# Start addresses of the high and low parts of a split-float matmul, moved to fixed remainders of 256 bytes

## The chip, the cores and the metric

The kernel runs on one core of one Trainium2 chip. The metric is the time of one execution in microseconds (us) on the device: 736.43 us is the median of three runs before the change (734.82 to 740.46). A core has 128 partitions of on-chip memory; every address below is a byte address within a partition, and "remainder" always means the address modulo 256.

## The reference

Two blocks of a network run one behind the other on 256 tokens of width 1024: a hybrid mixer with three attentions and a convolutional feed-forward, then a gated linear attention and a dilated window attention. Nearly all the arithmetic lies in products of the 256 x 1024 activations with weight matrices:

```python
z = h @ w_in                                      # first block, 6 + 24 column groups of 128..256
merged = gates0*(ya @ w_branch[0]) + ...          # three branches, then merged @ w_out
a, g = jnp.split(h @ w_up, 2, axis=-1)            # feed-forward, 2816 wide
y = (gelu(conv(a)) * g) @ w_down
proj = x @ gla_w_in;  out = (o * silu(g)) @ gla_w_out     # second block, first layer
kv = x @ w_kv;  proj = x @ swa_w_in;  out = (o * silu(g)) @ swa_w_out   # second layer
```

## The kernel before

**Split products.** A float32 operand is held as two tiles of a shorter float type that TensorE (PE) takes at full rate: a high part (the value rounded) and a low part (the rest). A product is then three matmuls, low x high, high x low and high x high, added up in the same accumulator; the low x low term is left out. `mm3` (line 265) issues these three; they are called a triple here. In a matmul one operand stands (its 128 x 128 block is loaded into the array first by a weight load, PEld, that runs while the matmul before it streams) and the other one moves (256 or 512 columns are streamed through).

**Weights.** `Stream` fetches each weight chunk (2048 floats a partition) by DMA into `raw`, and for each 1024 of them makes `whi` (ScalarE, ACT, line 158) and `wlo` (VectorE, DVE, line 159), each out of six rotating buffers. They are used in two ways:

- *Weights stand* (`wstat`, `wpair`, the first loop, `branch`): 128 x 128 blocks of `whi`/`wlo` stand, 256 columns of the activations move. The order of a triple is (`wlo` stands, high moves), (`whi` stands, low moves), (`whi` stands, high moves). Keys of such chunks are in the list `STILL`.
- *Weights move* (`tokmm`): 128 x 128 blocks of the activations stand, 512 columns of `whi`/`wlo` move. The order is (low stands, `whi` moves), (high stands, `wlo` moves), (high stands, `whi` moves).

**Activations.** The names are those of the trace: `hhi/hlo` (first mixer's input), `yhi/ylo` (attention outputs), `mhi/mlo` (merged), `h2hi/h2lo` (feed-forward's input), `fhi/flo` (its inner activations), `x2hi/x2lo` and `ohi/olo` (gated linear attention), `x3hi/x3lo` and `shi/slo` (window attention). `h`, `m`, `h2`, `x2` and `x3` come out of `big8` (line 397), which takes one of two buffers of the tag `big8r` and starts `past` floats into it. The triples are, by the loops:

| stage | moves or stands | triples |
|---|---|---|
| h: first loop 8 x 12, `inc` 16, `zg` 12 x 16 | moves, 256 columns | 304 |
| y: 3 branches x 8 x 2 | moves, 256 | 48 |
| h2: 22 `up` chunks x 16 | moves, 256 | 352 |
| x2: `gla` 8, four `gk` x 16 | moves, 256 | 72 |
| x3: three `kvk` x 16, sixteen `sq` x 16 | moves, 256 | 304 |
| m 32, f 88, x2 64, o 32, s 32 | stands, 512 weight columns move | 248 |
| x3: `kvv` | stands, 512 or 256 weight columns move | 32 |

**Where tiles lie.** A pool lays its tiles one behind the other; `Lines` rounds each tile up to whole 128 bytes. So a tile that is an odd multiple of 128 bytes long puts the next one at remainder 128. Before the change the `big8r` buffers are 8320 bytes (32.5 x 256): the first starts at remainder 0 and the second at 128. The `wlo` buffers are 4224 bytes (16.5 x 256): they start at 0 and 128 in turn, and where weights stand, 64 bytes further. `whi` buffers are 4096 bytes and all start at 0.

**Order.** The order of the instructions on each engine is set by the code's order, by priorities and by queues written out (`Queue`, `issue_after`). Semaphores tell an engine when a tile is ready or a buffer free.

Of the kernel before, what the change touches and what calls it, by code (L numbers as in the profile page):

```python
# [9 lines left out]
F32R = mybir.dt.float32r  # L10
# [8 lines left out]
S = 256  # L19
D = 1024  # L20
KK = 8
# [11 lines left out]
SC_SWA = float(128.0 ** -0.5)  # L33


STILL = ("in1", "inc", "zg", "br", "up", "gla", "gk", "kvk", "sq")

COLS = {}

# [63 lines left out]
class Stream:  # L103
# [31 lines left out]
    def _chunk(self, i):  # L135
        nc = self.nc
        key, ap, n, part = self.items[i]
        if part < 0:
            raw = self.early.tile([128, n], F32, tag="early", name="early", bufs=3)
        else:  # L140
            raw = self._raw()
        if not part:
            for o in range(0, n, 1024):
                nc.sync.dma_start(raw[:, o:o + 1024], ap[:, o:o + 1024])
            self.done.append(raw)
            return
        nc.sync.dma_start(raw[:, :n], ap)
        parts = []
        for o in range(0, n, part) if part > 0 else range(0, -part, 1024):
            m = min(part, n - o) if part > 0 else min(1024, -part - o)  # L150
            hi = self.pool.tile([128, 1024], F32R, tag="whi", name="whi", bufs=self.hlbufs)
            lo = self.pool.tile([128, 1056], F32R, tag="wlo", name="wlo", bufs=self.hlbufs)
            lo = lo[:, 16:1040] if key[0] in STILL else lo[:, 0:1024]
            with ExitStack() as st:
                for ins in self.behind:
                    st.enter_context(self.tc.issue_after(ins))
                st.enter_context(self.tc.high_priority(self.pri))
                i0 = nc.scalar.activation(hi[:, :m], raw[:, o:o + m], AF.Copy)  # L158
                i1 = nc.vector.tensor_sub(lo[:, :m], raw[:, o:o + m], hi[:, :m].bitcast(F32))  # L159
                self.last = (i0.ins, i1.ins)  # L160
            parts.append((hi, lo))
        self.done.append((part, parts) if part > 0 else (raw, (1024, parts)))
# [68 lines left out]
def hybrid_blocks(ctx, tc, A, out, dbg=None):  # L231
# [3 lines left out]
    cn = Lines(ctx.enter_context(tc.tile_pool(name="cn", bufs=1)), sm)  # L235
# [3 lines left out]
    def open_pool(name):  # L239
        st = ExitStack()  # L240
        p = st.enter_context(tc.tile_pool(name=name, bufs=1))
        return Lines(p, st.enter_context(tc.tile_pool(name=name + "s", bufs=1))), st.close
# [4 lines left out]
    def acc_t():  # L247

        return [ps.tile([128, 512], F32, tag="acc", name="acc", bufs=4) for _ in range(2)]

    def mm_t():
        return ps.tile([128, 512], F32, tag="mm", name="mm", bufs=2)
# [4 lines left out]
    def dump(name, t):  # L257
        if dbg and name in dbg:
            nc.gpsimd.dma_start(dbg[name], t)
# [135 lines left out]
            mm(pr[:, 256 + b:257 + b], ssq[:, b * 128:(b + 1) * 128], ones[:, 0:1], h == 0 and b == 0, h == 3, True)  # L395

    def big8(dt, name, past=0):
        t = cn.tile([128, KK * S + 32], dt, name=name, tag="big8r", bufs=2)
        return t[:, past:past + KK * S].rearrange("p (k s) -> p k s", k=KK)

    hT = (big8(F32R, "hhi"), big8(F32R, "hlo"))
    qk = [acc_t(), acc_t()]
    vps = [mm_t(), mm_t()]
    qci = [at_t(), at_t()]
# [105 lines left out]
    p1, close_p1 = open_pool("p1")  # L510
# [11 lines left out]
    def wpair(key, a, fresh=False):  # L522


        w = ws.get(key)
        p = mm_t()
        if fresh:
            for n in range(2):
                o = p[:, n * 256:(n + 1) * 256]
                W = [wsl(w, n * 1024 + k * 128, n * 1024 + (k + 1) * 128) for k in range(KK)]  # L530
                for k, l in enumerate(W):
                    mm(o, l[1], a[0][:, k, :], k == 0, False)
                    mm(o, l[0], a[0][:, k, :], False, False)
                for k, l in enumerate(W):
                    mm(o, l[0], a[1][:, k, :], False, k == KK - 1)
            return p
        for n in range(2):
            wstat(p[:, n * 256:(n + 1) * 256], w, n * 1024, a)
        return p
# [29 lines left out]
    p = wpair(("inc", 0), hT)  # L569
# [53 lines left out]
                               compare_op=OP.is_ge, fill=NEG, base=0, channel_multiplier=1)  # L623


    yT = (p1.tile([128, 6, S], F32R, name="yhi", tag="yhi"), p1.tile([128, 6, S], F32R, name="ylo", tag="ylo"))
    MC = {}
    hs = lambda h: (h % 2) * 2 + h // 2
    hb = lambda p, h, K: p[h % 2][:, h // 2 * 256:h // 2 * 256 + K]
# [146 lines left out]
    for i in range(2):  # L776
        w = ws.get(("br", i))
        for u in range(4):
            n = 4 * i + u
            p = mm_t()  # L780
# [6 lines left out]
        if i:  # L787
            w2 = ws.get(("br", 2))
            branch2(0)
            branch2(1)  # L790
        gates(9 + 2 * i)
    mT = (big8(F32R, "mhi"), big8(F32R, "mlo"))
    for i in range(4):
        if i > 1:
# [107 lines left out]

    close_p1()
    close_p1a()
    res, _ = open_pool("res")
    ctx.callback(_)
    p2, close_p2 = open_pool("p2")
    wk = p2
    xn = p2.tile([128, 2, D], F32, name="xn")
# [3 lines left out]

    rms_residual(y, xn, mod[0], x1, ORD1, (xr, mod[2]))
    dump("x1", x1)
    h2 = (big8(F32R, "h2hi"), big8(F32R, "h2lo", 16))

    def ev_h2(j, p, act, dve):
        for low in range(2):
# [76 lines left out]
    for i in range(4):  # L996
        p = wpair(("gk", i), x2T)
# [193 lines left out]
    xqt = p3.tile([128, 2, D], F32, name="lnw", tag="sg")  # L1191
    layer_norm(x2, y3, row("lng0"), None, x3, lambda i: (xkt, xqt)[i // 2][:, i % 2, :], ORD3)
    dump("x3", x3)
    x3T = (big8(F32R, "x3hi", 8), big8(F32R, "x3lo", 24))

    def ev_x3(j, p, act, dve):
        for low in range(2):
# [16 lines left out]
            nc.scalar.dma_start(x3d[b], x3[:, b, :])  # L1214

    close_p3()
    p4, close_p4 = open_pool("p4")
    ctx.callback(close_p4)
    wk = p4
# [3 lines left out]
    for i in range(3):  # L1223
        p = wpair(("kvk", i), x3T, i == 0)
# [84 lines left out]
    for h in range(8):  # L1309
# [8 lines left out]
        if h == 2:  # L1318
# [3 lines left out]
            for a in range(4):  # L1322
                for b in range(4):
                    q = (a % 2) * 64 + b * 16
# [119 lines left out]
```

## Time and profile before

| | |
|---|---|
| median of the runs | 736.43 us (734.82 to 740.46) |
| the profiled execution | 733.62 us, its span 731.6 us |
| PE busy | 700.6 us, 96% of the span |
| DVE, ACT, POOL busy | 547.1, 407.1, 20.2 us |
| mean granted clock of TensorE | 0.986 |

The profile's page sums busy time by engine. The timeline gives each matmul with its start and its duration; durations overlap, as matmuls are pipelined, so the pace of PE is the distance from one start to the next: the difference of two starts over the number of matmuls between them. The windows view gives busy time and the granted clock of a stretch. All starts are microseconds from the span's start.

### The profile page before, as it was taken

Reading aid. Unit: us, or ns where it says so; the run is one execution under the profiler, and the core shown is the slowest. Engines: PE = TensorE matmul, PEld = TensorE weight load, DVE = VectorE, ACT = ScalarE, POOL = GpSimd, SP = SyncE. Lnnn points to the kernel's source line nnn. Section 1 sums busy time; section 2 is a strip of 40 time slices with the busy share of each in tenths; the row PEclk is TensorE's granted clock in tenths of the full one; section 3 lists DMA queues with packets and bytes.
Section 4 is the critical chain, followed back from the end, with each engine's and each line's share of the span. In section 5 each row is a group of like instructions: output and inputs, shape, how many; then the busy total and the mean of one; then the engine's idle time right before and its main releaser. Section 6 shows DMA issues by size and latency. Waiting matters only on the chain. (4 is left out here: it accounts for less than half of the span.)

```text
span 731.6 us, 12192 instructions
## 1 busy us (share of the span) xinstructions
PE 700.6 (96%) x4878; PEld 636.4 (87%) x4878; DVE 547.1 (75%) x933; ACT 407.1 (56%) x675; POOL 20.2 (3%) x34
## 2 busy tenths in 40 slices
PE   4999999999979999999999899999989999999995
PEld 4888888998859999998999797888879999999984
DVE  5877969898868776768566756675777689777866
ACT  3447788546548555554545774543555556555542
POOL 0001000000010000000000200001010000000000
PEclk8999999999999999999999999999999999999999
DMA  8996768677734765758554464231437755433201
GB/s 321 418 345 237 275 257 301 229 250 255 256 136 174 276 243 178 262 207 310 201 195 174 181 224 141 109 116 58 189 142 276 261 194 168 168 125 135 89 1 57
DMA packets 24600, 148.74 MB, mean 203 GB/s; under 512 B 2992, under 2 KB 3248, under 8 KB 9568
## 3 DMA queue, kind: packets, MB, share of 16 engines
q1 hardware_dynamic: 21888, 139.05, 52.1%
q0 software_dynamic: 1280, 5.18, 2.1%
q10 hardware_dynamic: 1376, 3.74, 1.5%
q8 instruction: 38, 0.62, 0.3%
q14 instruction: 18, 0.15, 0.1%
HBM read 145.86 MB, written 2.10 MB: 202 GB/s over the span
## 5 line engine op out<-in xcount | busy, mean ns | idle before, releaser
L159 DVE TENSOR_TENSOR wlo<-raw,whi 128x1024 fp32r<-128x1024 f32 (+1 forms) x193 | 231.3, 1210 | 63.1 <-ACT whi L158 63.1
L158 ACT ACTIVATE whi<-raw 128x1024 fp32r<-128x1024 f32 (+1 forms) x193 | 199.4, 1050 | 94.1 <-PE acc L262 42.5
L262 PE MATMUL mm<-h2hi,wlo 128*128 128x256 f32 x352 | 98.3, 280 | 0.0
L262 PE MATMUL mm<-h2hi,whi 128*128 128x256 f32 x352 | 98.1, 280 | 0.0
L262 PE MATMUL mm<-h2lo,whi 128*128 128x256 f32 x352 | 97.0, 282 | 0.0
L262 PE MATMUL mm<-x3hi,wlo 128*128 128x256 f32 x304 | 86.2, 285 | 0.0
L262 PE MATMUL mm<-x3hi,whi 128*128 128x256 f32 x304 | 85.1, 281 | 0.0
L262 PE MATMUL mm<-x3lo,whi 128*128 128x256 f32 x304 | 82.9, 280 | 0.0
L262 PEld LDWEIGHTS mm<-h2hi,wlo 128*128 128x128 f32 x352 | 67.0, 190 | 0.4
L262 PEld LDWEIGHTS mm<-h2hi,whi 128*128 128x128 f32 x352 | 66.9, 190 | 0.0
L262 PEld LDWEIGHTS mm<-h2lo,whi 128*128 128x128 f32 x352 | 65.1, 188 | 0.3
L262 PE MATMUL mm<-hhi,wlo 128*128 128x256 f32 x208 | 59.5, 286 | 0.5 <-DVE wlo L159 0.3
L262 PE MATMUL mm<-hlo,whi 128*128 128x256 f32 x208 | 59.2, 285 | 0.0
L262 PE MATMUL mm<-hhi,whi 128*128 128x256 f32 x208 | 58.7, 282 | 0.0
L262 PEld LDWEIGHTS mm<-x3hi,wlo 128*128 128x128 f32 x304 | 57.7, 190 | 0.0
L262 PEld LDWEIGHTS mm<-x3hi,whi 128*128 128x128 f32 x304 | 57.5, 189 | 0.0
L262 PEld LDWEIGHTS mm<-x3lo,whi 128*128 128x128 f32 x304 | 56.2, 188 | 0.0
L262 PEld LDWEIGHTS mm<-hhi,wlo 128*128 128x128 f32 x208 | 39.0, 188 | 2.5 <-PE mm L262 0.8
L262 PEld LDWEIGHTS mm<-hlo,whi 128*128 128x128 f32 x208 | 39.1, 188 | 0.8 <-issue 0.8
L262 PEld LDWEIGHTS mm<-hhi,whi 128*128 128x128 f32 x208 | 39.1, 188 | 0.6 <-issue 0.5
L445 DVE SCALAR_TENSOR_TENSOR adacc<-raw,cact,adacc 128x1024 f32<-128x1024 f32 x28 | 35.7, 1276 | 0.2
L262 PE MATMUL acc<-whi,flo 128*128 128x512 f32 x88 | 34.8, 395 | 0.0
(355 smaller groups left out, 1604.0 us busy)
## 6 DMA issues: line engine op xcount, KB each, us to landing
raw<-in_w_up_dram SPq DMA_DIRECT2D x22, 1024.0 KB, 4.9
raw<-in_w_ada_dram SPq DMA_DIRECT2D x16, 1024.0 KB, 4.9
raw<-in_swa_q_dram SPq DMA_DIRECT2D x16, 1024.0 KB, 4.9
raw<-in_w_zg_dram SPq DMA_DIRECT2D x12, 1024.0 KB, 4.9
raw<-in_w_dn_dram SPq DMA_DIRECT2D x11, 1024.0 KB, 4.7
raw<-in_w_ada_dram SPq DMA_DIRECT2D x16, 512.0 KB, 9.0
early<-in_w_in_dram SPq DMA_DIRECT2D x8, 1024.0 KB, 7.3
raw<-in_gla_vg_dram SPq DMA_DIRECT2D x8, 1024.0 KB, 5.1
```

The lines of the kernel that those rows point to most:

```text
L158: i0 = nc.scalar.activation(hi[:, :m], raw[:, o:o + m], AF.Copy)
L159: i1 = nc.vector.tensor_sub(lo[:, :m], raw[:, o:o + m], hi[:, :m].bitcast(F32))
L262: return pe.matmul(o, l, r, start=start, stop=stop, skip_group_check=share)
L445: dve.scalar_tensor_tensor(a, w, c, a, op0=OP.mult, op1=OP.add)
```

## The change

High parts start at remainder 0 everywhere. Low parts of weights that stand start at remainder 64, low parts of activations that move at 192, all others at 0. For this the `wlo` buffers grow to 4352 bytes (17 x 256) and the `big8r` buffers to 8448 (33 x 256), so that every rotating buffer starts at the same remainder; `big8` gets the number of floats to start past (48, that is 192 bytes) for `h`, `h2` and `x3`; the `y` tiles get 256 bytes more, and their low part starts 192 bytes in. For room, the pool `res` (it holds `x2`, 8192 bytes) is closed before the pool of the last stage opens.

```diff
+PAST = 48
...
-            lo = self.pool.tile([128, 1056], F32R, tag="wlo", name="wlo", bufs=self.hlbufs)
+            lo = self.pool.tile([128, 1088], F32R, tag="wlo", name="wlo", bufs=self.hlbufs)
             lo = lo[:, 16:1040] if key[0] in STILL else lo[:, 0:1024]
...
     def big8(dt, name, past=0):
-        t = cn.tile([128, KK * S + 32], dt, name=name, tag="big8r", bufs=2)
+        t = cn.tile([128, KK * S + 64], dt, name=name, tag="big8r", bufs=2)
         return t[:, past:past + KK * S].rearrange("p (k s) -> p k s", k=KK)
 
-    hT = (big8(F32R, "hhi"), big8(F32R, "hlo"))
+    hT = (big8(F32R, "hhi"), big8(F32R, "hlo", PAST))
...
-    yT = (p1.tile([128, 6, S], F32R, name="yhi", tag="yhi"), p1.tile([128, 6, S], F32R, name="ylo", tag="ylo"))
+    yT = tuple(p1.tile([128, 6 * S + 64], F32R, name=n, tag=n)[:, q:q + 6 * S].rearrange("p (k s) -> p k s", k=6)
+               for n, q in (("yhi", 0), ("ylo", PAST)))
...
-    res, _ = open_pool("res")
-    ctx.callback(_)
+    res, close_res = open_pool("res")
...
-    h2 = (big8(F32R, "h2hi"), big8(F32R, "h2lo", 16))
+    h2 = (big8(F32R, "h2hi"), big8(F32R, "h2lo", PAST))
...
-    x3T = (big8(F32R, "x3hi", 8), big8(F32R, "x3lo", 24))
+    x3T = (big8(F32R, "x3hi"), big8(F32R, "x3lo", PAST))
...
     close_p3()
+    close_res()
     p4, close_p4 = open_pool("p4")
```

The remainders of the operands in the two built programs:

| stage | high, low of the activations before | after | `wlo` before | after |
|---|---|---|---|---|
| h (weights stand) | 0, 128 | 0, 192 | 64 and 192 in turn | 64 |
| y (weights stand) | 0, 0 | 0, 192 | 64 and 192 in turn | 64 |
| h2 (weights stand) | 0, 192 | 0, 192 | 64 and 192 in turn | 64 |
| x2 (weights stand) | 128, 0 | 0, 0 | 64 and 192 in turn | 64 |
| x3 (weights stand) | 32, 224 | 0, 192 | 64 and 192 in turn | 64 |
| m (weights move) | 128, 0 | 0, 0 | 0 and 128 in turn | 0 |
| x2 (weights move) | 128, 0 | 0, 0 | 0 and 128 in turn | 0 |
| f, o, s (weights move) | 0, 0 | 0, 0 | 0 and 128 in turn | 0 |
| x3 (weights move) | 32, 224 | 0, 192 | 0 and 128 in turn | 0 |

`whi` is at 0 before and after. Nothing is moved in the order: the rows of all five engines are the same in the two programs, and so are the semaphores and values that each instruction waits for and adds to.

## Rows read from the trace of the kernel before

**Rows 1.** The page: span, and busy time of each engine.

```profile
span 731.6 us, 12192 instructions
...
PE 700.6 (96%) x4878; PEld 636.4 (87%) x4878; DVE 547.1 (75%) x933; ACT 407.1 (56%) x675; POOL 20.2 (3%) x34
```

**Rows 2.** PE's waits, longest first: us in total, times, longest us.

```profile
PE acc L890 <- DVE x L193: 4.1, 3, 2.7
PE mm L262 <- DVE cact L373: 3.7, 1, 3.7
```

**Rows 3.** Windows of h2 with f, x3: stretch, us, busy (x count), PEclk, DMA share, GB/s.

```profile
238.00:395.00 157.00, 157.00 (x1139) 147.40 (x1138) 110.03 (x145) 81.86 (x113) 1.10 (x2) 1.00 0.64 228
...
542.00:594.00 52.00, 52.00 (x389) 49.86 (x388) 39.91 (x52) 32.20 (x46) 1.13 (x2) 0.98 0.72 249
594.00:700.00 106.00, 105.98 (x837) 102.83 (x836) 84.58 (x162) 62.45 (x103) 0.00 (x0) 1.00 0.38 134
```

**Rows 4.** Timeline, h2 stage (start us, us, instruction): first and last of 96 matmuls.

```profile
260.49 0.28 PE L262 MATMUL mm<-h2hi,wlo 128*128 128x256 f32 x1
...
271.48 0.28 PE L262 MATMUL mm<-h2hi,whi 128*128 128x256 f32 x1
```

**Rows 5.** Timeline, x3 stage: first and last of 144, then of 47 matmuls.

```profile
577.16 0.28 PE L262 MATMUL mm<-x3hi,wlo 128*128 128x256 f32 x1
...
594.02 0.28 PE L262 MATMUL mm<-x3hi,whi 128*128 128x256 f32 x1
...
639.10 0.28 PE L262 MATMUL mm<-x3lo,whi 128*128 128x256 f32 x1
...
644.53 0.28 PE L262 MATMUL mm<-x3hi,whi 128*128 128x256 f32 x1
```

**Rows 6.** Timeline, y stage: first and last of 47 matmuls.

```profile
144.61 0.28 PE L262 MATMUL mm<-ylo,whi 128*128 128x256 f32 x1
...
150.03 0.28 PE L262 MATMUL mm<-yhi,whi 128*128 128x256 f32 x1
```

**Rows 7.** Timeline, h stage: matmuls 1, 48, 50, 73 and 96 of 96.

```profile
150.15 0.28 PE L262 MATMUL mm<-hhi,wlo 128*128 128x256 f32 x1
...
155.58 0.28 PE L262 MATMUL mm<-hhi,whi 128*128 128x256 f32 x1
...
156.34 0.28 PE L262 MATMUL mm<-hlo,whi 128*128 128x256 f32 x1
...
159.10 0.28 PE L262 MATMUL mm<-hhi,wlo 128*128 128x256 f32 x1
...
161.81 0.28 PE L262 MATMUL mm<-hhi,whi 128*128 128x256 f32 x1
```

**Rows 8.** Timeline, x2 stage, weights stand: first and last of 165 matmuls.

```profile
418.89 0.28 PE L262 MATMUL mm<-x2hi,wlo 128*128 128x256 f32 x1
...
438.21 0.28 PE L262 MATMUL mm<-x2hi,whi 128*128 128x256 f32 x1
```

**Rows 9.** Timeline, f stage, weights move: first and last of 24 matmuls.

```profile
255.02 0.40 PE L262 MATMUL acc<-whi,flo 128*128 128x512 f32 x1
...
260.26 0.39 PE L262 MATMUL acc<-whi,fhi 128*128 128x512 f32 x1
```

**Rows 10.** Timeline, m stage, weights move: first and last of 94 matmuls.

```profile
191.43 0.40 PE L262 MATMUL acc<-whi,mhi 128*128 128x512 f32 x1
...
213.01 0.39 PE L262 MATMUL acc<-whi,mhi 128*128 128x512 f32 x1
```

**Rows 11.** Timeline, x2 stage, weights move: first and last of 24 matmuls.

```profile
438.33 0.39 PE L262 MATMUL acc<-whi,x2lo 128*128 128x512 f32 x1
...
443.65 0.40 PE L262 MATMUL acc<-whi,x2hi 128*128 128x512 f32 x1
```

**Rows 12.** Groups within 524.78:526.05, o stage, `wlo` at remainder 0: busy us, mean ns.

```profile
L262 PE MATMUL acc<-wlo,ohi 128*128 128x512 f32 x2 | 0.8, 389 | 0.0
```

**Rows 13.** Groups within 526.14:527.45, o stage, `wlo` at remainder 128.

```profile
L262 PE MATMUL acc<-wlo,ohi 128*128 128x512 f32 x2 | 0.8, 395 | 0.0
```

## The prediction

> **What bounds the kernel now.** I read the page first. PE is busy for 700.6 of 731.6 us [rows 1]; no other engine comes near. The waits view then says how much of the rest is waiting: the two longest entries of PE are 4.1 us and 3.7 us [rows 2], at a transition between layers and at the start, and the change touches neither. In the windows of the two stages with the most triples PE is busy without a gap: 157.00 of 157.00 us where h2 and f alternate, 52.00 of 52.00 and 105.98 of 106.00 us in x3 [rows 3]. So the time of these stages is the number of matmuls times the distance from one start to the next, and whatever shortens that distance comes off the end; there is no cover under which it could be lost.
>
> The distances are what the timeline is for. The reader is to see that they differ between stages in which the same instruction runs (128 x 128 standing, 256 moving columns):
>
> - h2: (271.48 - 260.49) / 95 = 115.7 ns [rows 4]
> - x3: (594.02 - 577.16) / 143 = 117.9 ns, and (644.53 - 639.10) / 46 = 118.0 ns [rows 5]
> - y: (150.03 - 144.61) / 46 = 117.8 ns [rows 6]
> - x2: (438.21 - 418.89) / 164 = 117.8 ns [rows 8]
>
> and, with 512 moving columns, f: (260.26 - 255.02) / 23 = 227.8 ns [rows 9], m: (213.01 - 191.43) / 93 = 232.0 ns [rows 10], x2: (443.65 - 438.33) / 23 = 231.3 ns [rows 11]. The clock does not make the difference: it is granted at 1.00, the upper level, in the h2 window and in the later x3 window alike [rows 3].
>
> **Why I put it down to addresses.** Within one stretch of the o stage, same instruction, same neighbours, the matmul that streams `wlo` takes 389 ns when the buffer starts at remainder 0 [rows 12] and 395 ns when it starts at 128 [rows 13]. Nothing else alternates there with the buffer. The size fits too: f, whose operands are all at 0 in this stretch, is the fastest of the moving-weight stages; m and x2, where the high part stands at 128, are the slow ones. With standing weights the layout (high 0, low 192, `wlo` 64 or 192) is h2's, and h2 is the fastest.
>
> [...]
>
> **The change part by part.** It removes, adds and moves no instruction, and no wait changes. What is left is the pace of each stage under its new remainders.
>
> - *x3, weights standing, 304 triples.* It gets h2's layout. At h2's pace a triple saves 3 x (117.9 - 115.7) = 6.6 ns; all 304 would save 2.0 us. The 48 `kvk` triples run in long stretches, and I give them all of it, 0.3 us. The 256 `sq` triples run in pieces of 48 matmuls with plain float32 matmuls between them, and the h stage shows that the pace after such a break depends on more than the addresses (next point). I give them two thirds of 256 x 3 x 2.3 ns = 1.8 us, 1.2 us. Together 1.5 us; bounds 0 and 2.1.
> - *h, 304 triples, low part from 128 to 192.* With unchanged addresses h shows three paces: (155.58 - 150.15) / 47 = 115.5 ns, then, after a wait, (159.10 - 156.34) / 23 = 120.0 ns with `wlo` at 64 and (161.81 - 159.10) / 23 = 117.8 ns with `wlo` at 192 [rows 7]. [...] If half the stretches run well and half as the mean of the two bad ones, 118.9, the stage runs at 117.2; all at h2's 115.7 would save 304 x 3 x 1.5 = 1.4 us, all at 120.0 would cost 304 x 3 x 2.8 = 2.6 us. h2 shows no bad stretch in its windows, but it is hardly ever broken up by float32 matmuls, so I take only 0.4 us.
> - *y, 48 triples, low part from 0 to 192.* 48 x 3 x (117.8 - 115.7) = 0.3 us at h2's pace; I take 0.2.
> - *x2, weights standing, 72 triples, high from 128 to 0, low at 0.* The nearest rows are y's, which has high and low at 0, and y runs at 117.8 like x2. I take 0; bounds 0 and 72 x 3 x 2.1 = 0.5 us.
> - *h2, 352 triples.* Only `wlo` changes, from 64 and 192 in turn to 64. The 96 matmuls of rows 4 hold both kinds and make one pace of 115.7. I take 0.
> - *m and x2, weights moving.* They get f's layout. m: 32 x 3 x (232.0 - 227.8) = 0.4 us. x2: 64 x 3 x (231.3 - 227.8) = 0.7 us. Bounds 0 and 1.1 for both.
> - *f, o, s.* About half of the 64 triples of o and s and a dozen of f's 88 have `wlo` at 128 now; each saves the 6 ns of rows 12 and 13: 44 x 6 = 0.3 us.
> - *x3, weights moving, 32 triples.* High goes from 32 to 0, low stands at 192, where none stood before. Between nothing and f's pace (the like of m, 0.4 us) I take 0.2.
> - *Tiles that only lie elsewhere.* `whi` and all behind `big8r` move by 256 bytes and more, the last pool by the freed 8192 bytes. No remainder of theirs changes and no wait is added: 0.
>
> Sum: 1.5 + 0.4 + 0.2 + 0.4 + 0.7 + 0.3 + 0.2 = 3.7 us. The profiled execution took 733.62 us and would take 729.9. It is 2.8 us below the median of the runs; the same 3.7 us off the median of 736.43 give **732.7 us**.
>
> **The rivals.**
>
> *Nothing happens* (736.4 us). [...] For it: the stages with high pace are those with float32 matmuls between. Against it: 577 to 594 us is a long stretch without such breaks and runs at 117.9 [rows 5], and the 389 and 395 ns alternate within one stretch. [...]
>
> *The new layout falls into the bad step* (slower). The h stage runs at 115.5 and at 120.0 with the same remainders, `wlo` at 64 among both; the change puts `wlo` at 64 in all stages. If x3, y and h, all broken up by float32 matmuls, settled at 120.0, it would cost 304 x 3 x 2.0 = 1.8 us in x3, 48 x 3 x 2.2 = 0.3 in y and 2.6 in h; the moving weights would still give back 1.6. That is 3.1 us slower, 739.5 us. It decides once these 656 triples run more than 1.6 us / 1968 = 0.8 ns slower than now. Against it: h2's fastest pace holds with `wlo` at 64 as well as at 192, and it has a distance of 64 between the streams where h has 128.
>
> *Every conflict goes* (much faster). With `wlo` at 0, f's distance of 227.8 for 512 columns is about 2 x 113.9. If x3, h, y and x2 ran at 113.9 for 256 columns, they would save 304 x 3 x 4.0 + 304 x 3 x 3.3 + 120 x 3 x 3.9 = 8.1 us, with 1.6 us of the moving weights 9.7 us: 726.7 us. Against it: h2 has this layout already and runs at 115.7.
>
> **How the numbers follow.** Forecast 0.72, nothing 0.12, bad step 0.09, much faster 0.07. The best bounds of the parts add up to 2.1 + 1.4 + 0.3 + 0.5 + 1.1 + 0.3 + 0.4 = 6.1 us, 730.3; the runs' median itself can lie a little lower, their lowest is 1.6 us under it, so the range begins at 729.3. Upwards it reaches over "nothing" to 736.5 and leaves out the bad step and the much faster case, 0.16 together. About 1%, 7.4 us, is what a measurement of this kernel can tell from no change. Faster by more than that takes the much faster case or a lucky median: 0.10. Slower by more than that takes more than the bad step: 0.03. The rest, 0.87, is within 1%.
>
> **What would show it right or wrong.** Right: the long x3 stretch near 575 to 592 us falls from 117.9 to about 115.7 ns, m and x2 with moving weights from 232 to about 228, h2 stays at 115.7, and the `wlo` matmuls of o take 389 ns in every buffer. The steps that could fail: the 48-matmul pieces of x3 may stay at 118 or go to 120 after their float32 breaks; h may go either way; the busy windows may be unchanged although the remainders are. The prediction as a whole is wrong if h2, whose layout stays, changes its pace, since then something other than the remainders of 256 matters (the 256-byte shift of `whi` against the activations, for one).

## The result and the profile after

The changed kernel takes 741.92 us (740.6 to 746.53, nine runs) against 736.9 us (734.82 to 740.46, nine runs) of the kernel before on the same chip: a ratio of 1.008 with a 95% interval of 1.0064 to 1.0097. It is 0.8% slower, 9.2 us above the predicted 732.7 and 5.4 us above the range's upper end. The profiled execution took 741.92 us with a span of 739.9. That is 8.3 us more span than before; 3.3 us of this belong to the profiled execution of before, which was that much shorter than the median of its runs, and 5.0 us are the difference of the medians.

The page, against [rows 1]: 8.6 us more busy time on PE with the same 4878 matmuls.

```profile
span 739.9 us, 12192 instructions
...
PE 709.2 (96%) x4878; PEld 646.1 (87%) x4878; DVE 547.3 (74%) x933; ACT 407.8 (55%) x675; POOL 20.1 (3%) x34
```

The longest waits of PE (us in total, times, longest us) are those of [rows 2] to the tenth, and all of PE's waits together come to 21.8 us, against 22.2 before. So the loss is not in the waits:

```profile
PE acc L893 <- DVE x L195: 4.1, 3, 2.7
PE mm L264 <- DVE cact L375: 3.7, 1, 3.7
```

The windows of the three stretches of [rows 3], shifted by what has accumulated: PE is still busy throughout, and the granted clock is 1.00 in all three.

```profile
242.00:402.00 160.00, 160.00 (x1130) 150.26 (x1129) 108.75 (x143) 81.91 (x113) 1.10 (x2) 1.00 0.62 222
550.00:601.00 51.00, 51.00 (x381) 48.50 (x381) 39.65 (x52) 31.75 (x45) 1.13 (x2) 1.00 0.71 249
601.00:709.00 108.00, 107.97 (x844) 104.74 (x843) 84.97 (x163) 62.72 (x104) 0.00 (x0) 1.00 0.37 132
```

So the time is again in the distances. The timeline (start us, us, instruction), as in [rows 4 to 11]:

h2, first and last of 96 matmuls: (275.66 - 264.25) / 95 = 120.1 ns, where [rows 4] gave 115.7. Nine of the ten long stretches of h2 run at 120.0 or 120.1; the first, which begins with another order of its matmuls, runs at 119.5 (before: 116.0 in the first, 115.7 in the others).

```profile
264.25 0.28 PE L264 MATMUL mm<-h2hi,wlo 128*128 128x256 f32 x1
...
275.66 0.28 PE L264 MATMUL mm<-h2hi,whi 128*128 128x256 f32 x1
```

x3, the long stretch of 144: (601.43 - 584.90) / 143 = 115.6 ns, where [rows 5] gave 117.9. Then twelve float32 matmuls, and the 47 behind the first: (608.94 - 603.42) / 46 = 120.0, where [rows 5] gave 118.0. The same tiles, the same remainders, and the first two `wlo` buffers of the two stretches are the very same ones (addresses 133696 and 129344 in the built program): two paces. The other long stretch of x3, 129 matmuls up to 568.02, runs at 119.5, where it ran at 117.7.

```profile
584.90 0.28 PE L264 MATMUL mm<-x3hi,wlo 128*128 128x256 f32 x1
...
601.43 0.28 PE L264 MATMUL mm<-x3hi,whi 128*128 128x256 f32 x1
601.55 1.92 PE L264 MATMUL at<-skT,sq 128*128 128x256 f32 x12
603.22 0.36 PE L264 MATMUL mm<-x3hi,wlo 128*128 128x256 f32 x1
603.42 0.28 PE L264 MATMUL mm<-x3lo,whi 128*128 128x256 f32 x1
...
608.94 0.29 PE L264 MATMUL mm<-x3hi,whi 128*128 128x256 f32 x1
```

y, 48 matmuls: (151.52 - 145.88) / 47 = 120.0, was 117.8 [rows 6]. h, the 48 behind it: (157.28 - 151.63) / 47 = 120.2, was 115.5 [rows 7].

```profile
145.88 0.28 PE L264 MATMUL mm<-yhi,wlo 128*128 128x256 f32 x1
...
151.52 0.28 PE L264 MATMUL mm<-yhi,whi 128*128 128x256 f32 x1
151.63 0.28 PE L264 MATMUL mm<-hhi,wlo 128*128 128x256 f32 x1
...
157.28 0.28 PE L264 MATMUL mm<-hhi,whi 128*128 128x256 f32 x1
```

m, 94 matmuls with moving weights: (215.08 - 193.97) / 93 = 227.0, was 232.0 [rows 10]. x2, 24 of them: (452.02 - 446.78) / 23 = 227.8, was 231.3 [rows 11]. x2 with standing weights, from 427.35 to 446.66 with 165 matmuls, stays at 117.7 [rows 8].

```profile
193.97 0.40 PE L264 MATMUL acc<-whi,mhi 128*128 128x512 f32 x1
...
215.08 0.39 PE L264 MATMUL acc<-whi,mhi 128*128 128x512 f32 x1
...
446.78 0.40 PE L264 MATMUL acc<-whi,x2lo 128*128 128x512 f32 x1
...
452.02 0.39 PE L264 MATMUL acc<-whi,x2hi 128*128 128x512 f32 x1
```

The o stage: the groups of lines within 532.60:534.00, and the same row word for word in the stretch behind it, 534.00:535.40. The 395 of [rows 13] has become the 389 of [rows 12] in both.

```profile
L264 PE MATMUL acc<-wlo,ohi 128*128 128x512 f32 x2 | 0.8, 389 | 0.0
```

The stages with moving weights thus did what was forecast. The loss lies where weights stand, and most of it in h2, the stage whose activations were left where they were.

### The profile page after: what moved, and what is told of

It reads as the page before. It is cut to its first block, busy times and chain, and to the rows that moved or that the text cites. A ratio compares the mean times of both kernels' runs of the same rounds, so it can differ in the third digit from the quotient of the medians.

```text
span 739.9 us, 12192 instructions
## 1 busy us (share of the span) xinstructions
PE 709.2 (96%) x4878; PEld 646.1 (87%) x4878; DVE 547.3 (74%) x933; ACT 407.8 (55%) x675; POOL 20.1 (3%) x34
## 5 line engine op out<-in xcount | busy, mean ns | idle before, releaser
L264 PE MATMUL mm<-h2hi,whi 128*128 128x256 f32 x352 | 100.0, 285 | 0.0
L264 PE MATMUL mm<-h2hi,wlo 128*128 128x256 f32 x352 | 99.9, 285 | 0.0
```

The source lines that it names most:

```text
L264: return pe.matmul(o, l, r, start=start, stop=stop, skip_group_check=share)
```

## The experiments

**How to read the tables.** A stage is the part of the kernel that multiplies one activation (h, y, h2 and so on). A pace is the distance from start to start in ns, taken over each stretch of at least 40 matmuls that nothing interrupts, and averaged over a stage's stretches. A pace of 115.7 is 347 ns a triple, 117.8 is 353, 120.0 is 360: steps of about 6.7 ns a triple. Layouts are written (high, low; `wlo`), remainders of the operands with standing weights; `whi` is always at 0. A ratio is the time over that of the kernel before, run alongside (medians 737.0, 737.35 and 738.28 us), with its 95% interval behind it. The granted clock is 1.00 around all lines of h2 shown.

### Undoing one part at a time

**Before, with `wlo` always at 64** (the activations stay as before; for room, the pool `res` is closed earlier, as in the change).

```diff
-            lo = self.pool.tile([128, 1056], F32R, tag="wlo", name="wlo", bufs=self.hlbufs)
+            lo = self.pool.tile([128, 1088], F32R, tag="wlo", name="wlo", bufs=self.hlbufs)
```

> The kernel before with one thing of the change: the low parts of standing weights start at remainder 64 in every buffer, no longer at 64 and 192 in turn (moving ones at 0 in every buffer; the pool res is closed early for room). Theory S (two steps): with these remainders the reads of the weights and of the activations can fall into a step of 347 ns a triple or one of 360 ns, and it was the buffers at 192 that pulled the bad step out; so h2 goes from 347 to about 360 ns a triple (+4.6 us), h partly too, and the kernel takes 740 to 743 us. Theory D (distance of 512): the 256-byte shift of the high weights against the high activations did it, which is not in this kernel; h2 stays at 347 ns a triple and the kernel takes 736 to 737 us.

741.66 us, ratio 1.0068 (1.0037 to 1.0099). Two lines of h2: (274.76 - 263.36) / 95 = 120.0 ns.

```profile
263.36 0.28 PE L262 MATMUL mm<-h2hi,wlo 128*128 128x256 f32 x1
...
274.76 0.28 PE L262 MATMUL mm<-h2hi,whi 128*128 128x256 f32 x1
```

The stages h, y and x3 keep their paces of before (117.0, 117.7, 117.9). So the edit to the `wlo` buffers makes h2 slow by itself. The time is in the range of "theory S", the two steps.

**After, with `wlo` at 192 instead of 64.**

```diff
-            lo = lo[:, 16:1040] if key[0] in STILL else lo[:, 0:1024]
+            lo = lo[:, 48:1072] if key[0] in STILL else lo[:, 0:1024]
```

> The changed kernel with the low parts of standing weights at remainder 192 in every buffer in place of 64. Theory S: with 192 the bad step can't hold where the low activations move from 192, h2, h, y and x3 go to about 347 ns a triple, and the kernel takes 729 to 733 us. Theory D: 192 or 64 is the same; h2 stays at 360 ns a triple and the kernel at 741 to 743 us.

733.6 us, ratio 0.9968 (0.9943 to 0.9993): faster than the kernel after, and 0.3% faster than the kernel before, just clear of the noise. h2 runs at (276.37 - 265.38) / 95 = 115.7, h at 115.8, y at 115.5, x3 at 115.6 and 116.1 in its long stretches and 116.0 in the pieces. With this one offset the terms of the prediction come true for x3, h and y.

```profile
265.38 0.28 PE L264 MATMUL mm<-h2hi,wlo 128*128 128x256 f32 x1
...
276.37 0.28 PE L264 MATMUL mm<-h2hi,whi 128*128 128x256 f32 x1
```

**After, with `wlo` at 64 and 192 in turn.**

```diff
+            self.n_lo = getattr(self, "n_lo", 0) + 1
+            s = 16 if self.n_lo % 2 else 48
-            lo = lo[:, 16:1040] if key[0] in STILL else lo[:, 0:1024]
+            lo = lo[:, s:s + 1024] if key[0] in STILL else lo[:, 0:1024]
```

> The changed kernel with the low parts of standing weights at 64 and 192 in turn, as before the change, and everything else as changed. Theory S: h2 goes back to 347 ns a triple, h, y and x3 to between 347 and 355, the kernel takes 730 to 735 us. Theory D: h2 stays at 360, the kernel at 741 to 743 us.

736.02 us, ratio 0.9998 (0.9968 to 1.0027), 1 us above the range expected, since h2 does not come all the way back. This run shows best what happens. In one stretch of h2, four buffers of 24 matmuls each stand at 64, 192, 64, 192; the rows are the first matmul of each and the last of all:

```profile
263.47 0.28 PE L266 MATMUL mm<-h2hi,wlo 128*128 128x256 f32 x1
...
266.35 0.28 PE L266 MATMUL mm<-h2hi,wlo 128*128 128x256 f32 x1
...
269.13 0.28 PE L266 MATMUL mm<-h2hi,wlo 128*128 128x256 f32 x1
...
271.90 0.28 PE L266 MATMUL mm<-h2hi,wlo 128*128 128x256 f32 x1
...
274.56 0.28 PE L266 MATMUL mm<-h2hi,whi 128*128 128x256 f32 x1
```

The first buffer, at 64, runs at (266.35 - 263.47) / 24 = 120.0 ns; the second, at 192, at 115.8; the third, at 64 again, at 115.4; the fourth at 115.7. The same remainder gives 120.0 or 115.4, by what ran ahead of it: with the buffer at 192 the pace becomes the good one, and the next buffer at 64 keeps it. Each of the eight stretches of four buffers between 246 and 377 us does the same, to 0.3 ns. In x3 the stretch of 144 and all ten pieces open with a buffer at 192, and there the buffers at 64 behind it run at about 115.6 throughout: (586.33 - 583.56) / 24 = 115.4 in the second buffer of the stretch of 144 (first matmuls of its first three buffers, at 192, 64 and 192):

```profile
580.78 0.28 PE L266 MATMUL mm<-x3hi,wlo 128*128 128x256 f32 x1
...
583.56 0.28 PE L266 MATMUL mm<-x3hi,wlo 128*128 128x256 f32 x1
...
586.33 0.28 PE L266 MATMUL mm<-x3hi,wlo 128*128 128x256 f32 x1
```

**After, with the high parts of h, h2 and x3 moved by 256 bytes** (so that their distance to `whi` modulo 512 is that of before).

```diff
-    h2 = (big8(F32R, "h2hi"), big8(F32R, "h2lo", PAST))
+    h2 = (big8(F32R, "h2hi", 64), big8(F32R, "h2lo", PAST))
```

and so for h and x3.

> The changed kernel with the high activations of h, h2 and x3 started 256 bytes later, which leaves every remainder of 256 as it is and gives back the distance of an odd multiple of 256 bytes between high weights and high activations that the kernel before had. Theory S: nothing changes, h2 at 360 ns a triple, 741 to 743 us. Theory D: h2 goes back to 347 ns a triple, and the kernel takes 732 to 737 us.

741.78 us, ratio 1.0063 (1.0038 to 1.0088), h2 at 120.0, x3's stretch of 144 at 115.7 and its pieces at 120.0, as after. The 256-byte shift that the prediction named as a possible other cause is not it.

### Mending h2 alone

The kernel after, with one line changed:

```diff
+            q_ = 48 if key[0] == "up" else 16
-            lo = lo[:, 16:1040] if key[0] in STILL else lo[:, 0:1024]
+            lo = lo[:, q_:q_ + 1024] if key[0] in STILL else lo[:, 0:1024]
```

> The kernel after with one stage mended: wlo at 192 for h2's chunks alone, 64 everywhere else. If the pace of h2 is the main term that the prediction left out, h2 goes from 360 to 347 ns, 352 x 13 = 4.6 us off 741.9, and 737.3 us, the time before, comes back; h, y and x3 stay at 357 to 360. Rival: the loss is spread over the stages that were broken up anyway, and h2's pace is made up elsewhere: 740 us or more.

737.77 us, ratio 1.0009 (0.9989 to 1.003). h2 (rows: first and last of 96) is back at (276.36 - 265.37) / 95 = 115.7 ns, and h, y and x3's pieces stay at 119.9, 120.1 and 119.7 (one of the ten pieces at 117.6).

```profile
265.37 0.28 PE L265 MATMUL mm<-h2hi,wlo 128*128 128x256 f32 x1
...
276.36 0.28 PE L265 MATMUL mm<-h2hi,whi 128*128 128x256 f32 x1
```

The offset of one stage's `wlo` buffers makes up the whole difference to the time before: by the ratios 1.0080 - 1.0009 = 0.7%, 5.2 us, where 4.6 were expected.

### Which layouts are good

Two accounts of the step were put to the test. "Differences": a triple has three pairs of operands (`wlo` with high, `whi` with low, `whi` with high), and two equal differences of their remainders make it slow. "Equal collides": each pair at one remainder costs a step of 6.7 ns. The edits set the offsets of `lo` in `_chunk` and of `big8`, as in the diffs above.

**`wlo` at 0, the low parts of h and h2 at 0 as well.**

> The kernel after, but the low part of standing weights starts at remainder 0, and the low parts of h and h2 at 0 too, so that all operands of h, h2 and x2 (728 triples with standing weights) stand at remainder 0; y and x3 keep (high 0, low 192) with wlo at 0. Theory 'equal remainders collide' (each pair read together at the same remainder costs about 6.7 ns a triple): all three pairs of h, h2 and x2 are equal, 360 ns a triple there, as h2 has now (x2 353 to 360); y and x3 have two equal pairs, 353 ns; time 740 to 742 us. Rival 'equal is free' (with moving weights all at 0 gives the fastest triple seen, 680 ns, twice 340): 340 ns in h, h2 and x2, that is 352 x 20 + 304 x 19 + 72 x 13 = 13.8 us off the time after, 728 us, less what x3 does.

743.36 us, ratio 1.0065 (1.0038 to 1.0092). h, h2 and x2, with all three pairs equal, run at 119.9; x3 and y, with two, at 117.9 and 118.2. These are the paces that "equal collides" forecast; the time is 1.4 us above its range. "Equal is free" falls, although with moving weights the same layout is the fastest seen (227 ns).

**`wlo` at 128.**

> The kernel after, but the low part of standing weights starts at remainder 128 (between 64, which gave 360 ns a triple in h2, and 192, which gave 347). Theory 'differences' (a triple reads three pairs together: wlo with high, whi with low, whi with high; it is slow when two of the three differences of start are the same and not 0): with wlo at 64 the differences are 64, 64 and 0, with 192 they are 192, 64 and 0, with 128 now 128, 64 and 0, all distinct, so 347 ns in h, h2, y and x3, and 733 to 734 us as with 192. Rival 'the remainder of wlo alone' (the nearer to 192 the better): about 353 ns, 737 to 738 us.

738.03 us, ratio 1.0009 (0.999 to 1.0027). h2, h and x3 run at 117.9, not at 115.7: "differences" falls here, and "equal collides" too, which counts one equal pair and says 347 ns. The rival "the remainder of `wlo` alone" said 353 ns and 737 to 738 us, and holds here.

**`wlo` at 64 and `wlo` at 192, with low at 64 in h and h2, at 128 in x3.**

> The kernel after with wlo at 64 as there, but the low parts of h and h2 at 64 and of x3 at 128 instead of 192. Theory 'differences': wlo-high 64, whi-low 192 (h, h2) or 128 (x3), whi-high 0, all distinct: 347 ns in h, h2 and x3, y stays at 360; 734 us. Rival 'the remainder of wlo alone': 64 is bad wherever the low part lies: 360 ns in h and h2, 357 in x3, 741 to 742 us as after.

> The mirror image: wlo at 192 as in the fast experiment, but the low parts of h and h2 at 64 and of x3 at 128. Theory 'differences': wlo-high 192 and whi-low 192 are the same again, so h and h2 go to 360 ns although wlo is at 192; x3 (192, 128, 0) and y (192, 64, 0) stay at 347: 733.6 + 352 x 0.013 + 304 x 0.012 = 741.8 us. Rival 'the remainder of wlo alone': 347 ns everywhere, 733.6 us.

736.77 us (0.998, 0.9959 to 1.0001) and 736.09 us (0.9983, 0.9959 to 1.0006). In both, h and h2 run at 117.8, where "differences" said 115.7 and 120.0 and "the remainder of `wlo` alone" 120.0 and 115.7. Both fall. Nor is x3 steady: its pieces run at 115.7 to 119.8 in the one and at 115.7 to 117.8 in the other.

**The high part off `whi`'s remainder.** Three maps, one profile each; `wlo` goes through 0, 64, 128 and 192 in four blocks of chunks in each stage.

```diff
+            q_ = {"up": key[1] * 4 // 22, "zg": key[1] // 3, "in1": key[1] // 2, "sq": key[1] // 4, "gk": key[1]}.get(key[0], 1) * 16
-            lo = lo[:, 16:1040] if key[0] in STILL else lo[:, 0:1024]
+            lo = lo[:, q_:q_ + 1024] if key[0] in STILL else lo[:, 0:1024]
```

> A map: the kernel after with the high part moved off whi's remainder. h stands at (high 64, low 64), h2 at (64, 128), x3 at (64, 192); wlo of standing weights goes through 0, 64, 128, 192 in four blocks of chunks within each stage. Theory 'equal remainders collide, 6.7 ns for each equal pair': in all layouts so far high and whi were both at 0, which is the one collision left in the fastest, 347 ns; with high at 64 no pair is equal unless wlo is at 64, so blocks with wlo at 0, 128 or 192 run at 340 ns a triple (3 x 113.3) and that with 64 at 347; the whole about 730 us. Rival 'what counts is how the three differences lie together': paces between 347 and 360 here as well, no block at 340, 735 to 742 us.

> The same map with h at (128, 128), h2 at (128, 192), x3 at (128, 64). 'Equal collides': 340 ns where wlo is at 0, 64 or 192, 347 with wlo at 128; about 730 us. Rival: 347 to 360 here too, 735 to 742 us.

> The same map with h at (192, 192), h2 at (192, 64), x3 at (192, 128). 'Equal collides': 340 ns where wlo is at 0, 64 or 128, 347 with wlo at 192; about 730 us. Rival: 347 to 360 here too, 735 to 742 us.

734.83, 741.76 and 738.78 us, one run each beside 738.11 of before. The distance from a triple's first matmul to the next triple's, median over a block of 54 to 93 triples (longer gaps than 400 ns left out):

| high, low | `wlo` 0 | 64 | 128 | 192 |
|---|---|---|---|---|
| 64, 64 (h) | 353 | 353 | 340 | 347 |
| 64, 128 (h2) | 353 | 354 | 360 | 351 |
| 64, 192 (x3) | 353 | 356 | 352 | 351 |
| 128, 128 (h) | 354 | 347 | 351 | 357 |
| 128, 192 (h2) | 358 | 353 | 350 | 354 |
| 128, 64 (x3) | 352 | 353 | 353 | 360 |
| 192, 192 (h) | 340 | 355 | 340 | 353 |
| 192, 64 (h2) | 353 | 353 | 353 | 353 |
| 192, 128 (x3) | 357 | 358 | 354 | 353 |

"Equal collides" falls: 27 of the 36 blocks (all with `wlo` not at high's remainder) have no equal pair, and only three of them are at 340. But those three are new: 340 is three times 113.3, half of what 512 columns take with moving weights, and no stage had run at it before. All three have high and low at the same remainder, 64 bytes to one side or the other of `whi`'s. A median can hide two paces in one block: the mean of these three is 343.7 with high at 192, twice, and 346.5 with high at 64.

### High and low both at 192

```diff
-    h2 = (big8(F32R, "h2hi"), big8(F32R, "h2lo", PAST))
+    h2 = (big8(F32R, "h2hi", PAST), big8(F32R, "h2lo", PAST))
```

and so for h, x3 and y; `wlo` at 0 in the one kernel, at 128 in the other (x2's at 192).

> High and low parts of h, h2, x3 and y all at 192, wlo of standing weights at 0 (192 for x2's two kinds of chunk). In the map, blocks of h with this layout had a median of 340 ns a triple and a mean of 343.7, as stretches after float32 breaks ran slower. If this is a property of the layout (the high and the low part stand alike, so the stream of moving columns runs on without a jump, and off whi), h2, which is hardly broken up, runs at 340, x3, h and y at about 344: against the kernel with wlo at 192 (347 ns) 352 x 7 + 656 x 3 ns = 4.4 us less, 729 us. Rival: it was the h stage's own breaks that set the step; h2 and x3 then stay at 347 to 355 and the time at 734 to 738 us.

> The same with wlo at 128 instead of 0, the other block of that stage with a median of 340. Layout theory: 340 in h2, about 344 in h, y and x3, 729 us, like the one with 0. Rival: 347 to 355, 734 to 738 us.

With `wlo` at 0: 733.28 us, ratio 0.9938 (0.9914 to 0.9963), between the two forecasts. Timeline of h2, its first stretch of 96 and its second, with the same remainders: (239.35 - 228.58) / 95 = 113.4 ns, then (256.11 - 244.92) / 95 = 117.8, and it stays there for the other eight. Good and bad step lie side by side in this layout. The two stretches read the same `wlo` and `whi` buffers in the same order (first addresses 124928, 116224, 111872 and 133632 for `wlo` in the built program), so no address of these operands differs between them.

```profile
228.58 0.28 PE L265 MATMUL mm<-h2hi,wlo 128*128 128x256 f32 x1
...
239.35 0.28 PE L265 MATMUL mm<-h2hi,whi 128*128 128x256 f32 x1
...
244.92 0.28 PE L265 MATMUL mm<-h2hi,wlo 128*128 128x256 f32 x1
...
256.11 0.28 PE L265 MATMUL mm<-h2hi,whi 128*128 128x256 f32 x1
```

With `wlo` at 128: **728.69 us, ratio 0.9874 (0.9839 to 0.9908)**, as the layout theory forecast (729), the best of all, 1.3% faster than before. A stretch of h2, first and last of 96: (269.36 - 258.55) / 95 = 113.8 ns.

```profile
258.55 0.29 PE L265 MATMUL mm<-h2hi,wlo 128*128 128x256 f32 x1
...
269.36 0.28 PE L265 MATMUL mm<-h2hi,whi 128*128 128x256 f32 x1
```

All its ten stretches are between 113.6 and 113.9, h is at 114.0, y at 113.4, x3 at 113.3 and 113.5 in the long stretches and 113.5 to 114.6 in the ten pieces. In this profile no start after a break falls into a worse step.

## Why the prediction was wrong

Its terms, and what the two traces hold. Both have the same 4878 matmuls in the same order, so each matmul's distance to the next can be compared one by one; "found" is the sum of these differences over a stage's matmuls. Left out are the single jumps of 0.08 us and more; most lie at a wait or where the granted clock is 0.50 in one of the two traces:

| term | forecast, us | found, us | by |
|---|---|---|---|
| x3, weights stand | -1.5 | +1.0 | stretch of 144 from 117.9 to 115.6 as forecast; the other long one 117.7 to 119.5; ten pieces 118.0 to 119.9 |
| h | -0.4 | +2.7 | 116.7 to 119.6, 912 matmuls |
| y | -0.2 | +0.2 | 118.1 to 120.0, 144 matmuls |
| x2, weights stand | 0 | 0 | 117.8 to 117.7 |
| **h2** | **0** | **+4.5** | 115.7 to 120.0, 1056 matmuls |
| m | -0.4 | -0.5 | 232.0 to 227.0, 96 matmuls |
| x2, weights move | -0.7 | -0.6 | 231.3 to 227.8 in the stretch of 24, 192 matmuls in all |
| f, o, s | -0.3 | -0.2 | o from 228.2 to 227.0; 389 ns in both `wlo` buffers of o looked at above; f itself +0.1 |
| x3, weights move | -0.2 | -0.1 | 96 matmuls |

The column, before rounding, adds up to +7.1 of the 8.3 us by which the two spans differ. The rest is the net of the jumps. The largest lies at the start of x2: 14 matmuls in a row start 213 ns apart instead of 118, 1.3 us more, at a granted clock of 0.50 where it was 1.00 before (first line below: before; second: after). In both kernels PE had waited for DVE three times just ahead of it, 1.03, 0.37 and 0.34 us before, 1.03, 0.38 and 0.34 after. Of the two traces with high and low at 192, that with `wlo` at 128 has such a row of matmuls too (eleven distances from 407.14 to 409.50 us, 214.5 ns each), that with `wlo` at 0 has not; that addresses cause it is not shown.

```profile
409.60:413.20 3.60, 3.26 (x27) 3.00 (x25) 3.54 (x5) 3.60 (x7) 3.31 (x5) 1.00 0.45 139
417.70:421.00 3.30, 3.26 (x15) 3.26 (x16) 3.30 (x5) 3.30 (x5) 2.75 (x4) 0.50 0.72 220
```

**The step that failed** is the one on h2's 352 triples: "Only `wlo` changes, from 64 and 192 in turn to 64. The 96 matmuls of rows 4 hold both kinds and make one pace of 115.7. I take 0." The observation was right and the inference was not. That a stretch with buffers at 64 and at 192 runs at one pace does not say that 64 alone would give this pace, since a pace can be kept from one buffer to the next. The prediction itself had said of the h stage that its pace after a break "depends on more than the addresses", and had shown 115.5, 120.0 and 117.8 ns there with unchanged addresses [rows 7]; it then read h2's mixture as if nothing but the addresses counted. The run with the two remainders in turn shows it within 11 us: 120.0, 115.8, 115.4, 115.7. Besides, "in turn" was loose: in the program of before, 240 of h2's 352 triples have `wlo` at 192 and 112 at 64. Every long stretch but the first opens with two buffers at 192, and the one at 64 comes third. So none of these stretches shows a buffer at 64 that opens one. The rows of h did show such a buffer, behind a wait, and it ran at 120.0 [rows 7]. The change took away the buffers at 192; with all of h2's at 192, and nothing else changed, 115.7 returns. The terms of x3, h and y rest on the same reading, since they took h2's 115.7 for a layout with `wlo` at 64 alone.

**The rival "the new layout falls into the bad step" was what happened** (the bad step is its pace of 120.0 ns, against 115.5 [rows 7]), and two things kept it too small and too unlikely. Its price covered x3, h and y, 3.1 us, and left out h2, the largest stage, which alone costs 4.5; the three came to 1.0 + 2.7 + 0.2 = 3.9 us, less than the 4.7 it had put for them. And the argument against it, "h2's fastest pace holds with `wlo` at 64 as well as at 192", is the same false reading. With h2 in it the rival would have come to 736.43 + 3.1 + 4.5 = 744.0 us, 2.1 us above the 741.9 measured, and the range would have had to hold it.

**The sign it had named.** It called itself wrong "if h2, whose layout stays, changes its pace, since then something other than the remainders of 256 matters". h2 did change. But its layout had not stayed, since `wlo` had moved, and `wlo` at 192 mends it; the shift by 256 bytes does nothing. What matters besides the remainders is what ran ahead.

**What was right.** Start addresses modulo 256 change the pace, and no wait does: fourteen further layouts of the same instructions ran between 728.7 and 743.4 us. The moving-weight terms came out within 0.1 us each. x2 with standing weights stayed where its nearest row, y, put it. And h2's old layout does bring x3, h and y to 115.5 to 116 ns, but reliably only with `wlo` at 192. That x3's stretch of 144 fell to 115.6 as forecast was luck: with the same remainders the other long stretch went to 119.5.

**"Every conflict goes"** (726.7 us) was refused because h2 had the new layout and ran at 115.7. That held for this layout; another one, high and low both at 192 and `wlo` at 128, does go to 113.3 to 114 in h, y, h2 and x3, and to 728.69 us.

**What stays open.** The runs give a table, not a rule. Three accounts of it (differences, equal remainders, `wlo` alone) fell. Why high and low at 192 with `wlo` at 128 has only the good step, why with `wlo` at 0 it has both, and what chooses between them at the start of a stretch, is not shown. That reads of the weights and of the activations fall into a step, as "theory S" has it, was the author's assumption: the runs show the paces, and nothing here measures the reads themselves, nor whether the writes of ACT and DVE to `whi` and `wlo` take part. And each layout has one trace, while its runs spread by 2.5 to 11 us where there are more than one; whether a stretch takes the same pace in every execution is not shown.

## What to carry to other kernels

When PE is busy without a gap and one stage still runs slower than another with the same instruction, compare the distances from start to start, then the operands' start addresses modulo 256. A pace read from a stretch that mixes two kinds of operand belongs to the mixture and to what ran ahead of it: a change that keeps only one kind is priced from a stretch that has only this kind, and where there is none, the worst pace seen with any of these remainders (here 120.0) is the price to put on every stage that gets them, the largest and the one "that stays as it is" first. Such a layout is then tried on the chip, stage by stage, since no rule found here gives its pace beforehand.

## What the hardware did that was not expected

- The long stretches of 128 x 128 x 256 matmuls of this type ran close to 113.3, 115.7, 117.8 or 120.0 ns from start to start, averaged over the stretch: steps of about 6.7 ns a triple, at a granted clock of 1.00. What was changed between the kernels is start addresses alone.
- The pace depended on what ran ahead. In h2 with `wlo` at 64 and 192 in turn, the good step was kept over a buffer of the other remainder (120.0, then 115.8, 115.4, 115.7), and the step differed between stretches that read the same buffers (113.4 and 117.8 in h2 with high and low at 192 and `wlo` at 0; 115.6 and 120.0 in x3 after).
- All operands at remainder 0 is the best layout seen with 512 moving weight columns (227 ns) and one of the worst with 256 moving activation columns (119.9 ns).
- The first of these matmuls behind x3's plain float32 ones took 603.42 - 603.22 = 0.20 us to the next start, some 80 ns more than its followers (lines of x3 in the profile after; 0.20 us in all ten places of that trace where 256 columns move behind `skT,sq`). The twelve rows of plain float32 ahead of it, twice 512 columns, took 603.22 - 601.55 = 1.67 us, some 0.84 us for 512 columns, where 512 columns of the split's type took 0.227 (m).
